# Zeros written by ScalarE, lambda powers placed by ScalarE copies, and one mask product for two heads

## The chip, the cores and the metric

The kernel runs on one core of a Trainium2 chip. Five engines work beside each other, each through its own queue in order: TensorE (PE, with its weight loads shown as PEld), VectorE (DVE), ScalarE (ACT), GpSimd (POOL) and SyncE (SP), which issues the DMAs. The metric is the device time of one execution in microseconds (us). The kernel before has a median of 950.24 us over three runs (948.44 to 950.54).

## The reference, cut to what matters

One decoder layer over 256 tokens of width 1024, in float32. The mixer makes one projection into S5 channels, q, k and v. Half of the channels go through a diagonal complex state space model, the other half through causal attention; their outputs meet in one output projection. Then follow a LayerNorm, a retrieval over 128 x 128 single-neuron experts (PEER), and a second LayerNorm.

```
proj = h @ w_in                                  # u | q | k | v
lam_bar = exp(lam * dt)                          # 32 groups x 64 complex states
bu = einsum('blgh,gph->blgp', u, b_bar)
states = scan(a1*a2, a2*b1 + b2)                 # over 256 tokens
y = real(einsum('blgp,ghp->blgh', states, c)) + d * u
y = gelu(y); y = y * sigmoid(y @ w_glu)
s = q @ k.T * scale;  s = where(k_pos <= q_pos, s, -1e30);  o = softmax(s) @ v
h = layernorm(alpha*h + concat(y, o) @ w_out)    # then PEER and a second layernorm
```

With 256 tokens and blocks of 256 there is only the own causal block, so the attention is plain causal attention over 8 heads of 64.

## The kernel before, in words

The tokens are permuted and stand in two blocks of 128 (b = 0 and 1). The S5 part works on chunks of 4 tokens: `Bbd` (128 x 2 x 16 x 4 x 32) holds the powers of lambda times B, and `Cbd` (128 x 2 x 16 x 5 x 32) those of lambda times C, both block diagonal over pairs of channel groups, so that zeros must stand off the diagonal. `Kin` (128 x 16 x 128) is the kernel within a chunk.

The mixer is a list of steps, `CFG["order"]` (line 46), emitted one after the other; a scheduler then sets the order on each engine. The steps that matter here are: `zero` (lines 666 to 671) fills `Bbd` on DVE, `Cbd` on POOL and `Kin` on ACT; `u` and `q` are projections whose products (lines 176 and 188) PE starts with; `par` makes the parameters on DVE, a long chain of operations on 128 x 16 tiles; `b` (from line 432) calls `powers` for `Bbd`; `min` (line 452) transposes `Bbd` on PE after the q projection; `c` calls `powers` for `Cbd`; `k` is the k projection as three products of split operands (`hi` and `lo`, lines 71 and 72); `e0`, `e1` (line 516) carry the inputs into chunk states; `v` (line 217) is the v projection in eight portions; `s0`, `s1` are the scans on DVE; `a0`, `a1` are `attend(0)` and `attend(1)`, four times each, with two heads a time; `kin` (line 498) makes `Kin`; `p0`, `p1` multiply with v; `o0`, `o1` read the states out; `glu` closes the S5 half.

`powers` forms, for the real and then the imaginary part, two products on DVE in full tiles (lines 421 and 422) and writes their difference or sum straight into the diagonal blocks, one instruction for each half of the partitions (line 426).

`attend` makes, for one of the two heads after the other, the score products (line 623: two recorded passes for each 128 x 128 block of keys) and adds the causal mask to the diagonal block by a product of an identity with the mask tile `mb` in bf16 (line 627). DVE takes the maximum (line 629), ACT the exponential (line 632), PE transposes the probabilities (line 637), ACT copies them out (line 639). The score banks (`pbank`) are four in number, the banks of the transposes (`abank`) two.

After the mixer come the output projection (line 768), the first LayerNorm, the retrieval's query products and the two long stages over the expert tables, in which PE works without a pause.

Of the kernel before, what the change touches and what calls it, by code (L numbers as in the profile page):

```python
# [14 lines left out]
AF = mybir.ActivationFunctionType  # L15
OP = mybir.AluOpType
# [6 lines left out]
NPAIR = 16  # L23
# [18 lines left out]
def f32(ap):  # L42
    return ap.bitcast(F32)


CFG = dict(order='mask zero u par b q min rt rot xs ks k c0 c vs e0 e1 s0 v v a0 v a0 v a0 a0 v s1 a1 v a1 v a1 a1 v kin p0 o0 p1 o1 glu',
           glu='VV',
           post='VV',
           yt='AAAAVVVVVVVPVVVV',
# [4 lines left out]
def layer(ctx, tc, I, out, tap=None, upto=None):  # L54
    nc = tc.nc
    V, S, P, PE = nc.vector, nc.scalar, nc.gpsimd, nc.tensor
# [24 lines left out]
    ident = const.tile([128, 128], F32, name="ident")  # L81
# [31 lines left out]
    with ExitStack() as px:  # L113
# [6 lines left out]
        with ExitStack() as mx:  # L120
# [14 lines left out]
            warm = se.tile([128, 512], F32, tag="yT", name="warm")  # L135
            V.memset(warm, 0.0)
            pt = pbank([128, 512])
# [30 lines left out]
            qk = sb.tile([128, 2, 4, T], F32, name="qk")  # L168
# [228 lines left out]
            Bbd = sb.tile([128, 2, NPAIR, 4, 32], F32, name="Bbd")  # L397
            Cbd = sb.tile([128, 2, NPAIR, 5, 32], F32, name="Cbd")
            MinT = sb.tile([128, 2, NPAIR, 128], F32, name="MinT")
            Kin = sb.tile([128, NPAIR, 128], F32, name="Kin")  # L400
            big = [se.tile([128, 1024], F32, name=f"big{n}") for n in range(4)]
            rot = sb.tile([128, 2, NPAIR, NCH], F32, name="rot")
# [5 lines left out]
            def powers(L, n, xr, xi, dst, k0, sg, EE, tmp):  # L408
                v = [b[:, :256 * n].rearrange("p (a k h) -> p a k h", k=n, h=16) for b in tmp]
                sh = [128, NPAIR, n, 16]  # L410
                lr, li = (L[:, i, :, :, None].to_broadcast(sh) for i in range(2))
                if sg < 0:
                    nl = sb.tile([128, NPAIR, n], F32, name="nl")
                    EE[1].tensor_scalar(nl, L[:, 0], -1.0, None, op0=OP.mult)
                    nlr = nl[:, :, :, None].to_broadcast(sh)
                xr, xi = (x[:, :, None, :].to_broadcast(sh) for x in (xr, xi))

                for i, (a, b) in enumerate(((xr, xi), (xi, xr))):
                    E = EE[i]
                    p, q = (v[(2 * i + k) % len(v)] for k in range(2))  # L420
                    E.tensor_tensor(p, a, nlr if i and sg < 0 else lr, op=OP.mult)
                    E.tensor_tensor(q, b, li, op=OP.mult)
                    for g in range(2):
                        sl = slice(64 * g, 64 * g + 64)
                        o = dst[sl, i, :, k0:k0 + n, 16 * g:16 * g + 16]
                        E.tensor_tensor(o, p[sl], q[sl],
                                        op=OP.add if i and sg > 0 else OP.subtract)

            bre, bim, cre, cim = (prm[:, 48 + 256 * n:304 + 256 * n].rearrange("p (a h) -> p a h", h=16)
                                  for n in range(4))  # L430
# [159 lines left out]
            mb = sb.tile([128, 128], BF, name="mb")  # L590
# [20 lines left out]
            def attend(b):  # L611

                nk = b + 1
                w = 128 * nk
                for n in range(4):

                    heads = [4 * (n // 2) + n % 2 + 2 * i for i in range(2)]
                    r = slice(64 * (n % 2), 64 * (n % 2) + 64)
                    pt = pbank([128, 2, T])
                    for i, h in enumerate(heads):  # L620
                        for kb in range(nk):
                            o = pt[:, i, 128 * kb:128 * kb + 128]
                            PE.matmul(o, qk[r, 0, h // 2, 128 * b:128 * b + 128],  # L623
                                      qk[r, 1, h // 2, 128 * kb:128 * kb + 128],
                                      start=True, stop=kb != b)
                            if kb == b:
                                PE.matmul(o, identb, mb, start=False, stop=True)
                    mx_ = sb.tile([128, 2], F32, tag="mx", bufs=2, name="mx_")
                    V.tensor_reduce(mx_, pt[:, :, :w], axis=AX.X, op=OP.max, negate=True)
                    p = sb.tile([128, 2, T], F32, tag="prob", bufs=2, name="p")  # L630
                    for i, h in enumerate(heads):
                        S.activation(p[:, i, :w], pt[:, i, :w], AF.Exp, bias=mx_[:, i:i + 1],
                                     accum_out=rs[:, b, h:h + 1])
                    pp = abank([128, 2, T])
                    for i in range(2):
                        for kb in range(nk):
                            PE.transpose(pp[:, i, 128 * kb:128 * kb + 128],
                                         p[:, i, 128 * kb:128 * kb + 128], ident)
                    S.copy(pTs[b][:, n], pp[:, :, :w])
                    yield  # L640
# [23 lines left out]

            def do(w):
                if w == "zero":
                    V.memset(Bbd, 0.0)
                    P.memset(Cbd, 0.0)
                    P.memset(Rt[:, :, 0:1], 0.0)
                    S.activation(Kin, ident[:, None, :].to_broadcast([128, NPAIR, 128]), AF.Copy,  # L670
                                 scale=0.0)
                elif w == "u":
                    pu = [abank([128, 512]) for _ in range(2)]
                    tokproj(0, pu)
                    for b in range(2):
                        V.transpose(U[:, :, b, :], pu[b].rearrange("p (a g) -> p a g", g=32))
                elif w == "q":
                    M["q"] = chproj(1, 0.125, lambda q: [(w_in(1, q), xT)])
                elif w == "k":
                    def parts(q):  # L680
                        hi, lo = M["wk", q]
                        return (hi, mixh), (hi, mixl), (lo, mixh)
                    chproj(2, 1.0, parts)
                elif w == "ks":
                    for q in range(4):
                        M["wk", q] = split(load(I["w_in"][2, :, 2 * q:2 * q + 2, :]), V)
                elif w == "vs":
                    vsplit()
                elif w == "xs":
                    xsplit()  # L690
                elif w == "v":

                    if "pv" not in M:
                        M["pv"] = [sbank([128, 512]) for _ in range(2)]
                        M["vproj"], M["left"] = vproj(M["pv"]), 8
                    next(M["vproj"])
                    M["left"] -= 1
                    if not M["left"]:
                        M["v"] = vn = sb.tile([128, 2, 512], F32, tag="vn", name="vn")
                        for b in range(2):  # L700
                            S.copy(vn[:, b], M["pv"][b])
                elif w == "par":
                    M["p"] = s5_params()
                elif w == "b":
                    s5_b(M["p"][0])
                elif w == "c0":
                    s5_c0()
                elif w == "c":
                    s5_c()
                elif w == "rt":  # L710
                    s5_rt(M["p"][1])
                elif w == "rot":
                    s5_rot()
                elif w == "min":
                    with tc.issue_after(M["q"].ins):
                        s5_min()
                elif w == "kin":
                    s5_kin()
                elif w in ("e0", "e1"):
                    M[w] = s5_e(int(w[1]))  # L720
                elif w in ("s0", "s1"):
                    if "S" not in M:
                        M["S"] = sb.tile([128, 2, NPAIR, NCH + 1], F32, tag="MinT", name="Sst")
                        P.memset(M["S"][:, :, :, 0:1], 0.0)
                    s5_scan(int(w[1]), M["e" + w[1]], M["S"])
                elif w in ("o0", "o1"):
                    if "y" not in M:
                        M["y"] = se.tile([128, 4, 2, 4, 32], F32, tag="yT", name="yT")
                    s5_out(int(w[1]), M["S"], M["y"])
                elif w == "mask":  # L730
                    masks()
                elif w in ("a0", "a1"):
                    if w not in M:
                        M[w] = attend(int(w[1]))
                    next(M[w])
                elif w in ("p0", "p1"):
                    values(int(w[1]), M["v"])
                elif w == "glu":
                    glu(M["y"])
                else:  # L740
                    raise ValueError(w)
# [101 lines left out]
            for q in range(4):  # L843
                raw = stream.tile([128, 1024], F32, tag="raw", bufs=RAWB, name="raw")
                for k in range(2):
                    c = 256 * q + 128 * k
# [518 lines left out]
```

## Time and profile before

| what | value |
|---|---|
| median of three runs | 950.24 us |
| the profiled execution's own time | 949.19 us |
| its span, from the first to the last instruction | 947.4 us |
| mean granted TensorE clock, as a share of full speed | 0.995 |
| PE busy | 935.1 us, 99% of the span |
| DVE, ACT and POOL busy | 722.2, 562.7 and 11.2 us |

Busy shares are means over stages with different limits. The first 125 us, to the end of the mixer, are the part that the change touches; DVE is nearly full there between 20 and 80 us. A TensorE matmul's end is modelled, so that rows of one engine overlap; the time from one row's start to the next one's start is what a step takes. A float32 product is recorded as two passes.

### The profile page before, as it was taken

What the parts mean: (1) busy time and instruction counts of PE and PEld (TensorE: products, weight loads), DVE (VectorE), ACT (ScalarE), POOL (GpSimd) and SP (SyncE); (2) the same over time, 40 slices, a digit from 0 to 9 for tenths busy, and PEclk for the clock granted to TensorE, in tenths of its full rate; (3) what the DMA queues carried; (4) which work ended last, traced back from release to release, by engine and by line L of the source; (5) the groups of instructions that cost most, each with busy time, mean ns of one, the idle gap of its engine ahead of it and who ended that gap; (6) DMA issues with size and microseconds to landing.
All of it is one profiled execution on the core that took longest, in us unless ns stands there. A gap on an engine that the chain in (4) does not pass through costs nothing.

```text
span 947.4 us, 15310 instructions
## 1 busy us (share of the span) xinstructions
PE 935.1 (99%) x5591; PEld 810.3 (86%) x5591; DVE 722.2 (76%) x1495; ACT 562.7 (59%) x1067; POOL 11.2 (1%) x19
## 2 busy tenths in 40 slices
PE   9999999999999999999999999999999999999996
PEld 4987889998888888999999999888888888888875
DVE  9998687998988967888898996655555555555566
ACT  4526544566575667998888776554455465445550
POOL 3000010000000000000000000000000000000000
PEclk9999999999999999999999999999999999999998
DMA  7331573455555555354444445555555575555561
GB/s 290 111 113 57 172 239 112 135 179 202 195 181 198 182 196 176 130 186 156 156 157 156 157 157 178 197 189 193 197 193 189 196 286 186 195 198 191 191 198 45
DMA packets 50075, 166.18 MB, mean 175 GB/s; under 512 B 5328, under 2 KB 9936, under 8 KB 49872
## 3 DMA queue, kind: packets, MB, share of 16 engines
q1 hardware_dynamic: 50000, 165.20, 51.7%
q8 instruction: 44, 0.72, 0.3%
q14 instruction: 31, 0.25, 0.1%
HBM read 163.09 MB, written 2.10 MB: 174 GB/s over the span
## 4 chain that ended last, share of the span: by engine, by line
PE 95%; DVE 4%; issue 0%; DMA 0%; ACT 0%; DVEq 0%; ACTq 0%
PE pg L1180 35%; PE pw L916 16%; PE pw L1268 10%; PE pw L918 10%; PE pg L1141 3%; PE pa L1268 3%; PE pw L919 2%; PE pw L768 2%; PE pw L188 2%; PE pa L176 2%; PE psb L217 1%; PE pa L871 1%; PE pw L623 1%; PE pw L498 1%; PE psb L552 1%; PE pw L648 1%
## 5 line engine op out<-in xcount | busy, mean ns | idle before, releaser
L72 DVE TENSOR_TENSOR lo<-raw,hi 128x1024 fp32r<-128x1024 f32 x167 | 204.4, 1224 | 150.7 <-ACT hi L71 150.4
L71 ACT CAST hi<-raw 128x1024 fp32r<-128x1024 f32 x167 | 175.9, 1054 | 169.6 <-PE pg L1180 153.9
L1180 PE MATMUL pg<-hi,wv 128*128 128x512 f32 x980 | 262.5, 389 | 0.5 <-ACT wv L1110 0.5
L1180 PEld LDWEIGHTS pg<-hi,wv 128*128 128x128 f32 x980 | 183.8, 188 | 39.0 <-ACT wv L1110 0.9
L916 PE MATMUL pw<-x,hi 128*128 128x512 f32 x672 | 171.2, 393 | 0.0
L1180 PE MATMUL pg<-lo,wv 128*128 128x512 f32 x490 | 151.1, 389 | 0.0
L916 PEld LDWEIGHTS pw<-x,hi 128*128 128x128 f32 x672 | 124.3, 189 | 23.2
L79 DVE TENSOR_TENSOR lo<-raw,hi 128x1024 fp32r<-128x1024 f32 x96 | 117.1, 1220 | 16.8 <-ACT hi L78 15.8
L918 PEld LDWEIGHTS pw<-x,lo 128*128 128x128 f32 x768 | 104.8, 190 | 7.4
L1180 PEld LDWEIGHTS pg<-lo,wv 128*128 128x128 f32 x490 | 92.0, 188 | 19.2
L918 PE MATMUL pw<-x,lo 128*128 128x256 f32 x768 | 107.3, 282 | 0.0
L78 ACT CAST hi<-raw 128x1024 fp32r<-128x1024 f32 x96 | 101.2, 1054 | 3.8 <-PE pa L1268 2.7
L921 ACT COPY ul<-pw 128x256 f32<-128x256 f32 x96 | 35.6, 371 | 90.0 <-PE pw L919 90.0
L1135 ACT ACTIVATE o<-eq,gL 128x128 f16<-128x128 f16 x256 | 84.3, 440 | 6.0 <-DVE eq L1131 5.6
L1268 PEld LDWEIGHTS pw<-x,hi 128*128 128x128 f32 x512 | 65.9, 189 | 1.3
L1268 PE MATMUL pw<-x,hi 128*128 128x256 f32 x512 | 66.6, 283 | 0.0
L1110 ACT CAST wv<-act 128x256 fp32r<-128x256 f32 x124 | 51.9, 419 | 0.8 <-DVE act L1147 0.8
L1111 DVE TENSOR_TENSOR wv<-act,wv 128x256 fp32r<-128x256 f32 x124 | 51.7, 418 | 0.0
L1268 PE MATMUL pw<-x,lo 128*128 128x256 f32 x256 | 38.8, 292 | 0.0
L919 PE MATMUL pw<-x,hi 128*128 128x512 f32 x96 | 38.0, 396 | 0.0
L1141 PE MATMUL pg<-o,o 128*128 128x128 f16 x512 | 36.5, 219 | 0.0
L922 DVE TENSOR_TENSOR us<-pw,ul 128x256 f32<-128x256 f32 x64 | 26.8, 418 | 11.6 <-ACT ul L921 10.9
(349 smaller groups left out, 1129.6 us busy)
## 6 DMA issues: line engine op xcount, KB each, us to landing
raw<-in_u SPq DMA_DIRECT2D x128, 512.0 KB, 3.5
raw<-in_v SPq DMA_DIRECT2D x128, 512.0 KB, 4.3
raw<-in_w_q SPq DMA_DIRECT2D x12, 512.0 KB, 4.3
raw<-in_w_in SPq DMA_DIRECT2D x8, 512.0 KB, 6.4
raw<-in_w_out SPq DMA_DIRECT2D x8, 512.0 KB, 4.2
w<-in_w_in SPq DMA_DIRECT2D x7, 512.0 KB, 9.4
raw<-in_w_q SPq DMA_DIRECT2D x8, 256.0 KB, 5.0
raw<-in_w_glu SPq DMA_DIRECT2D x2, 512.0 KB, 3.4
```

What stands on the lines that cost most here:

```text
L71: S.copy(hi, raw)
L72: eng.tensor_tensor(lo, raw, f32(hi), op=OP.subtract)
L78: S.copy(hi, raw)
L79: return hi, lo, V.tensor_tensor(lo, raw, f32(hi), op=OP.subtract)
L916: PE.matmul(pt, hi[:, 128 * d:128 * d + 128], x2[:, d], start=d == 0, stop=False)
L918: PE.matmul(pt[:, 0], lo[:, 128 * d:128 * d + 128], xh[:, d], start=False, stop=False)
L919: PE.matmul(pt, hi[:, D - 128:], x2[:, ND - 1], start=False, stop=True)
L1110: S.copy(wh, of_tile(half, i))
L1135: S.activation(o2[:, 1, i // 2, :, i % 2], eq[:, i // 2, :, i % 2], AF.Copy, scale=gL[:, t0 + i:t0 + i + 1])
L1141: PE.matmul(pt[:, i], o1[:, i // 2, :, i % 2], o2[:, k, i // 2, :, i % 2], start=k == 0, stop=k == 1)
L1180: PE.matmul(acc[b][:, c], x[:, tk], w[:, 512 * c:512 * c + 512], start=first and j == 0, stop=last and j == 2)
L1268: PE.matmul(pt, w[:, 128 * d:128 * d + 128], x[:, d], start=n == 0 and d == 0, stop=n == 2 and d == ND - 1)
```

## The change

`Bbd`, `Kin` and `Cbd` are filled by ACT copies from `warm`, a tile of zeros; the memset of `Bbd` leaves DVE and that of `Cbd` leaves POOL, and the fill of `Kin` no longer reads `ident`. The fill of `Cbd` is a step of its own (`zc`). In `powers` DVE makes one subtraction or addition over all partitions in place, and ACT copies the two halves into the diagonal blocks. In `attend` one mask product over both heads (128 x 2 x 128) comes first and opens the accumulation, and the score products of the diagonal block follow on top of it.

```diff
-CFG = dict(order='mask zero u par b q min rt rot xs ks k c0 c vs e0 ...
+CFG = dict(order='mask zero u par b q min rt rot xs zc ks k c0 c vs e0 ...
...
                     E.tensor_tensor(q, b, li, op=OP.mult)
+                    E.tensor_tensor(p, p, q, op=OP.add if i and sg > 0 else OP.subtract)
                     for g in range(2):
                         sl = slice(64 * g, 64 * g + 64)
-                        o = dst[sl, i, :, k0:k0 + n, 16 * g:16 * g + 16]
-                        E.tensor_tensor(o, p[sl], q[sl],
-                                        op=OP.add if i and sg > 0 else OP.subtract)
+                        S.copy(dst[sl, i, :, k0:k0 + n, 16 * g:16 * g + 16], p[sl])
...
-                    for i, h in enumerate(heads):
-                        for kb in range(nk):
-                            o = pt[:, i, 128 * kb:128 * kb + 128]
-                            PE.matmul(o, qk[r, 0, h // 2, 128 * b:128 * b + 128],
+                    for kb in range(nk):
+                        if kb == b:
+                            PE.matmul(pt[:, :, 128 * b:128 * b + 128], identb,
+                                      mb[:, None, :].to_broadcast([128, 2, 128]), start=True, stop=False)
+                        for i, h in enumerate(heads):
+                            PE.matmul(pt[:, i, 128 * kb:128 * kb + 128],
+                                      qk[r, 0, h // 2, 128 * b:128 * b + 128],
                                       qk[r, 1, h // 2, 128 * kb:128 * kb + 128],
-                                      start=True, stop=kb != b)
-                            if kb == b:
-                                PE.matmul(o, identb, mb, start=False, stop=True)
+                                      start=kb != b, stop=kb != b or i == 1)
...
                 if w == "zero":
-                    V.memset(Bbd, 0.0)
-                    P.memset(Cbd, 0.0)
+                    for z in (Bbd, Kin):
+                        o = z.rearrange("p a b c d -> p (a b c d)") if z is Bbd else z.rearrange("p a b -> p (a b)")
+                        S.copy(o.rearrange("p (n c) -> p n c", c=512),
+                               warm[:, None, :].to_broadcast([128, o.shape[1] // 512, 512]))
                     P.memset(Rt[:, :, 0:1], 0.0)
-                    S.activation(Kin, ident[:, None, :].to_broadcast([128, NPAIR, 128]), AF.Copy,
-                                 scale=0.0)
+                elif w == "zc":
+                    o = Cbd.rearrange("p a b c d -> p (a b c d)")
+                    S.copy(o.rearrange("p (n c) -> p n c", c=512),
+                           warm[:, None, :].to_broadcast([128, 10, 512]))
```

The scheduler moves instructions with it, up to the end of the mixer; behind that the order on every engine is the same. Three places follow.

On ACT at the start of the program, before:

```order
L670 ACT_TABLE_LOAD
L670 ACTIVATE Kin_127<-ident_61 128x2048
L199 CAST mixh_87<-x0_96 128x512
L485 COPY Rt_133<-pw_120 128x16x63
L199 CAST mixh_87<-x0_96 128x512
L378 COPY LamB_123<-Lam_122 128x32
L199 CAST mixh_87<-x0_96 128x512 x2
```

and in the changed kernel:

```order
L671 ACT_TABLE_LOAD
L671 COPY Bbd_124<-warm_98 128x4096
L671 COPY Kin_127<-warm_98 128x2048
L676 COPY Cbd_125<-warm_98 128x5120
L378 COPY LamB_123<-Lam_122 128x32 x2
L484 COPY Rt_133<-pw_120 128x16x63
L378 COPY LamB_123<-Lam_122 128x32
L199 CAST mixh_87<-x0_96 128x512 x4
```

Three fills of 4096, 2048 and 5120 columns stand in a row, and the copies of lambda and the casts of x come behind all three.

On PE behind the products of `e0` and `e1`, where before eight pairs of a score product and a mask product stood in a row (the last two and the first v products are shown; `psb` is the bank of the v projection):

```order
L627 LDWEIGHTS identb
L627 MATMUL pw<-mb,identb 128x128
L623 MATMUL pw<-qk 128x128
L627 LDWEIGHTS identb
L627 MATMUL pw<-mb,identb 128x128
L217 MATMUL psb<-hi,mixh 128x512
L217 MATMUL psb<-hi,mixl 128x512
L217 MATMUL psb<-lo,mixh 128x512
```

the changed kernel has:

```order
L515 MATMUL pa<-U,MinT 128x64 x16
L217 MATMUL psb<-hi,mixh 128x512
L217 MATMUL psb<-hi,mixl 128x512
L217 MATMUL psb<-lo,mixh 128x512
L217 MATMUL psb<-hi,mixh 128x512
L217 MATMUL psb<-hi,mixl 128x512
L217 MATMUL psb<-lo,mixh 128x512
L622 LDWEIGHTS identb
L622 MATMUL pw<-mb,identb 128x2x128
L625 MATMUL pw<-qk 128x128 x2
L217 MATMUL psb<-hi,mixh 128x512
L217 MATMUL psb<-hi,mixl 128x512
```

The v products now come first, and the four blocks of b = 0 (one mask, two scores) stand between them.

On ACT in the attention of b = 1 (`p` is a pair's probabilities, `vn` the copy of v, `x0` takes the transposed probabilities, `W5` is a tile of the output weights), before:

```order
L632 ACTIVATE p_769,rs_136<-pw_760,mx__767 128x256 x2
L701 COPY vn_850<-psb_658 128x512
L639 COPY x0_96<-pa_772 128x512
L632 ACTIVATE p_793,rs_136<-pw_784,mx__791 128x256 x2
L632 ACTIVATE p_817,rs_136<-pw_808,mx__815 128x256 x2
```

and in the changed kernel:

```order
L633 ACTIVATE p_768,rs_136<-pw_760,mx__766 128x256 x2
L71 CAST W5_1157<-raw_1158 128x1024
L640 COPY x0_96<-pa_771 128x512
L633 ACTIVATE p_791,rs_136<-pw_783,mx__789 128x256 x2
L633 ACTIVATE p_814,rs_136<-pw_806,mx__812 128x256 x2
```

The copy of v stood behind the first pair's exponentials; now the cast of `W5` stands there, which overwrites q and k and so waits for PE's last score product, and the copies of v come later.

## Rows read from the trace of the kernel before

**Rows 1.** The page: busy time of the engines, share of the span, instructions.

```profile
PE 935.1 (99%) x5591; PEld 810.3 (86%) x5591; DVE 722.2 (76%) x1495; ACT 562.7 (59%) x1067; POOL 11.2 (1%) x19
```

**Rows 2.** The waits of PE between 0 and 175 us: who waited for whom, us in total, times, the longest.

```profile
PE pa L1268 <- DVE lo L961: 0.6, 1, 0.6
PE psb L579 <- DVE yl L571: 0.4, 1, 0.4
PE psb L578 <- ACT yh L570: 0.3, 1, 0.3
```

**Rows 3.** The table of stretches: length, busy time of PE, PEld, DVE, ACT and POOL with instructions in brackets, granted clock, DMA share, GB/s.

```profile
55.00:60.00 5.00, 5.00 (x34) 3.90 (x32) 4.96 (x6) 1.05 (x1) 0.15 (x1) 1.00 0.49 143
60.00:65.00 5.00, 5.00 (x18) 3.82 (x18) 5.00 (x8) 0.00 (x0) 0.00 (x0) 0.66 0.50 172
75.00:80.00 5.00, 5.00 (x31) 3.51 (x29) 4.61 (x8) 3.49 (x16) 0.00 (x0) 1.00 0.00 0
```

**Rows 4.** PE in order of time in the k projection: start us, modelled duration us, what.

```profile
46.44 0.28 PE L188 MATMUL pw<-mixl,hi 128*128 128x256 f32 x1
46.80 0.39 PE L188 MATMUL pw<-mixh,lo 128*128 128x256 f32 x1
47.03 0.28 PE L188 MATMUL pw<-mixh,hi 128*128 128x256 f32 x1
```

**Rows 5.** PE in order of time, scores and masks of b = 0, then the first v products.

```profile
57.15 0.23 PE L627 MATMUL pw<-mb,identb 128*128 128x128 bf16 x1
57.30 0.48 PE L623 MATMUL pw<-qk 64*128 64x128 f32 x2
57.72 0.23 PE L627 MATMUL pw<-mb,identb 128*128 128x128 bf16 x1
...
61.22 0.56 PE L217 MATMUL psb<-hi,mixh 128*128 128x512 f32 x1
...
62.43 0.63 PE L217 MATMUL psb<-hi,mixh 128*128 128x512 f32 x1
62.86 0.63 PE L217 MATMUL psb<-hi,mixl 128*128 128x512 f32 x1
...
64.95 0.39 PE L217 MATMUL psb<-hi,mixh 128*128 128x512 f32 x1
65.18 0.40 PE L217 MATMUL psb<-hi,mixl 128*128 128x512 f32 x1
```

**Rows 6.** PE in order of time, one pair of heads of b = 1 and the v products behind it.

```profile
69.88 0.71 PE L623 MATMUL pw<-qk 64*128 64x128 f32 x4
70.52 0.23 PE L627 MATMUL pw<-mb,identb 128*128 128x128 bf16 x1
70.68 0.71 PE L623 MATMUL pw<-qk 64*128 64x128 f32 x4
...
71.36 0.48 PE L217 MATMUL psb<-wv,mixh 128*128 128x512 f32 x1
71.67 0.41 PE L217 MATMUL psb<-wv,mixl 128*128 128x512 f32 x1
```

**Rows 7.** DVE in order of time: the fill of `Bbd`, two of the first parameter operations, and the first operation of step `b`.

```profile
2.20 3.47 DVE L667 MEMSET Bbd<- 128x4096 f32 x1 [0.80 <-issue]
...
6.36 1.49 DVE L245 TENSOR_SCALAR pw<-pw 128x16 f32<-128x16 f32 x1
...
8.70 0.17 DVE L245 TENSOR_SCALAR pw<-pw 128x16 f32<-128x16 f32 x1
...
19.12 0.41 DVE L436 TENSOR_TENSOR big<-prm,pw 128x256 f32<-128x256 f32 x1
```

**Rows 8.** POOL in order of time.

```profile
1.93 4.36 POOL L668 MEMSET Cbd<- 128x5120 f32 x1
...
6.29 1.53 POOL L748 IOTA iotaq<- 128x256 f16 x1
7.76 0.46 POOL L750 IOTA iotal<- 128x256 bf16 x1
```

**Rows 9.** The parameters' first DMA on SP (start us, us) and, from the list of DMA issues up to 60 us, size and us from issue to landing.

```profile
1.65 0.42 SPq L146 DMA_DIRECT2D prm<-in_prm  x1
prm<-in_prm SPq DMA_DIRECT2D x1, 24.0 KB, 2.5
```

**Rows 10.** ACT's table load, its fill of `Kin` and two placing copies of half the partitions, and DVE's placing of powers in `Bbd`, in order of time.

```profile
0.74 1.28 ACT L670 ACT_TABLE_LOAD   x1 [0.74 <-PEq L1354]
10.38 1.91 ACT L670 ACTIVATE Kin<-ident 128x2048 f32<-128x2048 f32 x1 [8.36 <-DVE ident L96]
23.31 0.82 ACT L444 COPY Bbd<-Bc 64x256 f32<-64x256 f32 x2 [1.92 <-DVE Bc L441]
28.55 1.91 DVE L426 TENSOR_TENSOR Bbd<-big,big 64x768 f32<-64x768 f32 x2
```

**Rows 11.** PE's first transposes of `Bbd`; ACT in the attention of b = 1, a copy of transposed probabilities and the second pair's first exponential; PE's transposes of one pair's probabilities.

```profile
33.49 1.04 PE L452 MATMUL psb<-ident,Bbd 128*128 128x128 f32 x8
81.58 0.59 ACT L639 COPY x<-pa 128x512 f32<-128x512 f32 x1
82.06 0.49 ACT L632 ACTIVATE p<-pw,mx__791 128x256 f32<-128x256 f32 x1
80.90 0.60 PE L637 MATMUL pa<-ident,p 128*128 128x128 f32 x4
```

More of the change, by code (lines that the diff above doesn't have):

```diff
@@ L43, in f32 @@
     return ap.bitcast(F32)
-CFG = dict(order='mask zero u par b q min rt rot xs ks k c0 c vs e0 e1 s0 v v a0 v a0 v a0 a0 v s1 a1 v a1 v a1 a1 v kin p0 o0 p1 o1 glu',
+CFG = dict(order='mask zero u par b q min rt rot xs zc ks k c0 c vs e0 e1 s0 v v a0 v a0 v a0 a0 v s1 a1 v a1 v a1 a1 v kin p0 o0 p1 o1 glu',
            glu='VV',
```

## The prediction

> **What bounds the kernel now.** I read the page first: PE is busy 99% of the span, every other engine less [rows 1]. The list of PE's waits comes second. Up to 175 us, past its start, it holds only three short ones, 0.6, 0.4 and 0.3 us [rows 2]. So PE is the bound nearly everywhere, and DVE and ACT count only where they make PE wait. Busy time does not show steps that are longer than they need be; for that I read, third, the table of stretches, where the granted clock is 0.66 between 60 and 65 us, while PE is busy all the time [rows 3]; and fourth, PE in order of time, measuring from one start to the next. The reader is to see three things there.
>
> First, in the k projection one step takes 46.80 - 46.44 = 0.36 us and the next 0.23, where its neighbours take 0.12 (47.03 to the next row and the rows ahead show it as an even beat): 0.24 + 0.10 = 0.34 us are a short wait for `lo`, which DVE makes late [rows 4]. Second, the v products step by 62.86 - 62.43 = 0.43 us at first and by 65.18 - 64.95 = 0.23 later; that is the lower of the clock's two levels (1.2 GHz) against the upper (2.4 GHz) [rows 5]. Third, a score product behind a mask takes 57.72 - 57.30 = 0.42 us for its two passes, a mask 57.30 - 57.15 = 0.15, together 0.57 for a head of b = 0 [rows 5]; with four passes (b = 1) the scores take 0.64 and the head 70.68 - 69.88 = 0.80 [rows 6]. Two more passes thus cost only 0.22: half of the 0.42 is the change between score and mask.
>
> **The change part by part.** The sum is made against the profiled execution, 949.19 us (span 947.4), which is 1.05 us under the median of 950.24.
>
> *One mask for two heads.* Eight of 16 masks go. A pair of b = 0 costs 2 x 0.57 = 1.14 now. Then it is a mask, a score behind a mask (0.42) and one behind a score (0.22). A mask of 256 columns is not in the trace; it is at least the 0.15 of 128 columns, and at most 0.21 if 128 more columns cost a quarter of the 0.23 us that 512 take. That is 0.79 to 0.85, a gain of about 0.3 each. A pair of b = 1 costs 71.36 - 69.88 = 1.48 now; then 0.64 for the two heads' first block of keys, and 0.79 to 0.85 less the 0.1 that is saved where no mask follows the last score: 1.33 to 1.39, a gain of about 0.1. Four of each: 4 x 0.3 + 4 x 0.1 = 1.6. Against that stand the changes between v products and scores: the four b = 0 blocks now stand at three places instead of one (the order shows it), and the first v step behind scores is 71.67 - 71.36 = 0.31 rather than 0.23 [rows 6]; with the way in I take 0.05 to 0.15 for each of two more. I take 1.5 in all; bounds -0.3 (nothing gained in the pairs, the switches paid) and 2.9 (0.36 for each of eight).
>
> *The clock.* The v products from 61.22 to 65.18 are ten steps in 3.96 us; at 0.23 they would be 2.3, so 1.7 us are lost [rows 5]. What PE did before the clock fell was eight pairs of score and mask in a row, half of the rows of the array in use (64*128). The stretch ahead, 55 to 60 us, has 1.00, and so has the one with b = 1 scores, from 75 to 80 [rows 3]. In the changed order v products at 512 columns stand ahead of and between the b = 0 blocks, and the blocks are denser. I take the fall as gone: 1.7; bounds 0 (it stays) and 1.7. The Trainium skill ("TensorE: Matmul & The Clock Gate", HAM oscillation — how this bites in real kernels) has gaps in which PE idles bring the clock down. By that rule the fall has no cause here, since PE is busy throughout, and the edit could not remove it: the sum would be 1.8 instead of 3.5. The trace differs from it, with 5.00 of 5.00 us busy at a clock of 0.66, so I go by the order of the work.
>
> *Zeros.* DVE's memset of 3.47 us goes, POOL's of 4.36 too [rows 7, 8]. DVE's parameter chain now starts at 2.20 + 3.47 = 5.7 us, behind the memset, and its first operations are stretched: one of 16 columns takes 1.49 us where a like one takes 0.17, and ends at 7.85, just as POOL's iota does (6.29 + 1.53 = 7.82) [rows 7, 8]. In the changed kernel POOL is through with its iotas at about 4 us (1.93, where the memset started, + 1.53 + 0.46), and the parameters land at 1.65 + 2.5 = 4.15 [rows 9]. So the chain runs from 4.15 without a stretch, and step `b` starts at about 15 instead of 19.12 us: DVE is 4 us ahead. On ACT the fills cost 1.91 / 2048 us a column [rows 10]: 3.8 + 1.9 + 4.8 = 10.5 us from the end of the table load at 2.02, so to 12.5 us; now the fill of `Kin` ends at 12.3, because it waits for `ident`. Nothing is late by it. Cost nothing; without that cover the copies of lambda would take from DVE's 4 us, not from PE.
>
> *Powers.* DVE saves half of its placing, 1.91 / 2 for each of two parts of `Bbd` [rows 10], and for `Cbd` 4/3 of that, having 1024 columns for 768: 1.9 + 2.5 = 4.4 us. ACT gets eight copies of 64 partitions; a placing of 256 columns takes 0.82 / 2 = 0.41 [rows 10], and with 512 and 768 more columns at the fill's rate they take 0.9 and 1.1, together 8 us. ACT has room: 1.05 us busy of 5 from 55 to 60, 0 from 60 to 65 [rows 3]. For PE `Bbd` must be whole at 33.49 [rows 11]; today DVE ends it at 30.46, then, 4 us earlier with a copy of 1.8 behind, at about 28. Cost nothing; if the cover of 5 us went, each further microsecond would be PE's. DVE then reaches `lo` in the k projection some 4 us earlier, and the wait of 0.34 goes. What is late next is PE itself.
>
> *ACT's queue in the attention.* The cast of `W5` (1.05) now waits for PE's last score product, and behind it stand a copy of 0.48 (82.06 - 81.58 [rows 11]) and the second pair's exponentials of 0.45. They reach PE 2.0 us after the last score. PE has four transposes (0.60 with a modelled end [rows 11], so 0.4 to 0.6), six v products (6 x 0.23) and two of `kin` (as the two passes of a score, 0.22 each, an estimate) until it needs them: 2.2 to 2.4. It fits by 0.2 to 0.4 us. Cost nothing; if it slips, up to 1.
>
> *Downstream.* The order behind the mixer is the same. The two waits of 0.4 and 0.3 in `glu` [rows 2] hang on the end of the S5 output, which moves with PE; they stay.
>
> Sum: 1.5 + 1.7 + 0.34 = 3.5. 949.19 - 3.5 = 945.7 for an execution like the profiled one; with the 1.05 to the median, 946.7.
>
> **The rivals.**
>
> *The clock still falls*, at the same place or at another one. For it: PE was never idle before, so I know only one instance of the cause; the b = 0 blocks still end with two in a row. Against it: the v products between. 950.24 - 1.8 = 948.4.
>
> *The gain is given back at the end of the mixer.* PE comes 3.5 us earlier to `glu` and the output projection, and finds weights or the chain from S5 output to `yl` not ready. For it: PE already waits there, on DVE and ACT [rows 2]. Against it: those loads are issued when DVE has finished with a buffer, and DVE is ahead. 950.2, no change.
>
> *ACT becomes the bound at the end of the attention.* The cast stands at the head of the queue and three pairs wait behind it. If PE had to wait for each pair's copy and exponentials in full (0.48 + 0.9), that is 3 x 1.4 + 1.05 = 5.2 us, and in such a lull the clock could fall, 1.7 more: 950.24 - 3.5 + 6.9 = 953.6. It decides from 3.5 us of such waiting on; against it stand the 0.2 to 0.4 us of room, and that all four pairs' score banks are filled by then.
>
> **How the numbers follow.** Forecast 0.62, clock falls 0.17, given back 0.12, ACT bound 0.09. A measurement of this kernel tells 0.2% from no change, 1.9 us: faster is under 948.34, slower over 952.14. The forecast is faster in nine of ten of its cases (its own spread is that of the mask, about 1 us, and of the runs, about 1), the clock case lies on the bound and is faster in half. Faster: 0.56 + 0.085 = 0.65; slower 0.09; the same 0.26. The range: best case 2.9 + 1.7 + 0.34 = 4.9 and the lowest run 1.8 below the median give no more than 943.5; above it reaches past the given-back case, 950.6, and leaves out the slower one.
>
> **What would show it.** Right: eight mask rows of 128x256 with steps near 0.8 us for a block of b = 0; a clock of 1.00 in all stretches from 55 to 70 us; step `b` on DVE at about 15 us; an even beat of 0.12 in the k projection; the last score product some 3.5 us earlier, and the output projection as well. Wrong: PE waits on the exponentials or on `Bbd`, a lower clock anywhere in the mixer, or an output projection that starts where it did.

## The result and the profile after

The changed kernel takes 945.33 us (median of five runs, 945.16 to 945.89) where the kernel before, run beside it, takes 950.44 (948.44 to 950.67). The ratio is 0.9949, with a 95% interval of 0.9938 to 0.9961: 5.1 us, or 0.5%, faster. The prediction was 946.7 us, so the direction and the range held and the time came out 1.4 us lower. The two profiled executions stand closer: 949.19 against 945.52, a gain of 3.67 where 3.5 was forecast. Why the medians are further apart than the profiles is the question of one of the experiments; in a later comparison the medians were 949.24 (15 runs) and 945.50, 3.7 us apart.

The page of the changed kernel: the span, and busy time, share and instructions of each engine, which answer to [rows 1].

```profile
span 943.7 us, 15299 instructions
PE 931.6 (99%) x5583; PEld 807.3 (86%) x5583; DVE 712.9 (76%) x1490; ACT 578.1 (61%) x1077; POOL 6.9 (1%) x18
```

PE has eight products fewer, the eight masks. DVE lost 9.3 us and ACT gained 15.4, and neither difference is in the time as such.

The waits of PE between 0 and 175 us in the changed kernel, which answer to [rows 2]:

```profile
PE pa L1274 <- DVE lo L967: 0.6, 1, 0.6
PE psb L578 <- DVE yl L570: 0.4, 1, 0.4
PE psb L577 <- ACT yh L569: 0.3, 1, 0.3
```

They are the same three with the same sizes; no new wait has come. The table of stretches of the changed kernel (busy PE, PEld, DVE, ACT, POOL, granted clock, DMA share, GB/s), beside [rows 3]:

```profile
55.00:60.00 5.00, 5.00 (x29) 4.07 (x29) 5.00 (x8) 0.00 (x0) 0.16 (x1) 1.00 0.50 190
60.00:65.00 5.00, 5.00 (x26) 3.53 (x25) 3.46 (x8) 3.27 (x9) 0.00 (x0) 1.00 0.01 3
```

The 0.66 between 60 and 65 us has become 1.00. PE in order of time in the changed kernel (start, modelled duration): its first product at line 188, the k projection, the first v product, the first block of b = 0, the last two, a pair of b = 1 followed by v products, two pairs of b = 1 one behind the other, and the first product of the output projection.

```profile
19.41 1.67 PE L188 MATMUL pw<-x,w 128*128 128x256 f32 x7
...
46.78 0.28 PE L188 MATMUL pw<-mixh,hi 128*128 128x256 f32 x1
46.90 0.28 PE L188 MATMUL pw<-mixl,hi 128*128 128x256 f32 x1
...
56.00 0.48 PE L217 MATMUL psb<-hi,mixh 128*128 128x512 f32 x1
...
57.46 0.28 PE L622 MATMUL pw<-mb,identb 128*128 128x256 bf16 x1
57.67 0.71 PE L625 MATMUL pw<-qk 64*128 64x128 f32 x4
58.31 0.50 PE L217 MATMUL psb<-hi,mixh 128*128 128x512 f32 x1
58.65 0.39 PE L217 MATMUL psb<-hi,mixl 128*128 128x512 f32 x1
...
63.53 0.28 PE L622 MATMUL pw<-mb,identb 128*128 128x256 bf16 x1
...
64.38 0.28 PE L622 MATMUL pw<-mb,identb 128*128 128x256 bf16 x1
...
66.83 0.71 PE L625 MATMUL pw<-qk 64*128 64x128 f32 x4
...
68.32 0.50 PE L217 MATMUL psb<-wv,mixh 128*128 128x512 f32 x1
...
73.88 0.71 PE L625 MATMUL pw<-qk 64*128 64x128 f32 x4
74.52 0.28 PE L622 MATMUL pw<-mb,identb 128*128 128x256 bf16 x1
74.73 0.72 PE L625 MATMUL pw<-qk 64*128 64x128 f32 x8
75.39 0.28 PE L622 MATMUL pw<-mb,identb 128*128 128x256 bf16 x1
...
76.24 0.44 PE L638 MATMUL pa<-ident,p 128*128 128x128 f32 x2
...
105.32 0.39 PE L774 MATMUL pw<-hi,mixh 128*128 128x512 f32 x1
```

The reader is to see five things. The k projection keeps its beat of 0.12. A mask for two heads takes 57.67 - 57.46 = 0.21, a block of b = 0 64.38 - 63.53 = 0.85. The first v step behind scores takes 58.65 - 58.31 = 0.34. A pair of b = 1 followed by v takes 68.32 - 66.83 = 1.49, no less than the 1.48 of [rows 6]; two pairs one behind the other take 76.24 - 73.88 = 2.36, and the eight score passes that stand between their masks take 75.39 - 74.73 = 0.66, where four take 74.52 - 73.88 = 0.64. And the output projection starts at 105.32.

The kernel before, PE in order of time, at the same two ends and at three marks between them (the first score of b = 0, a mask of b = 1 ahead of v, the first v product behind the last score):

```profile
19.67 1.24 PE L188 MATMUL pw<-x,w 128*128 128x256 f32 x5
...
56.73 0.49 PE L623 MATMUL pw<-qk 64*128 64x128 f32 x2
...
71.32 0.23 PE L627 MATMUL pw<-mb,identb 128*128 128x128 bf16 x1
...
80.12 0.48 PE L217 MATMUL psb<-hi,mixh 128*128 128x512 f32 x1
...
108.96 0.42 PE L768 MATMUL pw<-hi,mixh 128*128 128x512 f32 x1
```

From the first product at line 188 to the output projection both kernels do the same work but for the eight masks. That length, called the stretch from here on, leaves out the start, where PE waits for the first weights by a different amount in each execution. It was 108.96 - 19.67 = 89.29 us and is 105.32 - 19.41 = 85.91: 3.38 of the 3.67 us. Behind it nothing changed.

DVE, POOL and ACT in order of time in the changed kernel: DVE's first parameter operation and the first product of step `b` (at line 435), POOL's two operations that stood behind its memset, ACT's fills, the last placing in `Bbd`, and the cast of `W5` (recorded as `W`) with what follows it.

```profile
4.17 0.17 DVE L245 TENSOR_SCALAR pw<-prm 128x16 f32<-128x16 f32 x1 [2.77 <-DMA prm<-in_prm]
...
15.41 0.43 DVE L435 TENSOR_TENSOR big<-prm,pw 128x256 f32<-128x256 f32 x1
```

```profile
1.99 1.53 POOL L754 IOTA iotaq<- 128x256 f16 x1
3.46 0.46 POOL L756 IOTA iotal<- 128x256 bf16 x1
```

```profile
2.03 3.60 ACT L671 COPY Bbd<-warm 128x4096 f32<-128x4096 f32 x1
5.54 1.89 ACT L671 COPY Kin<-warm 128x2048 f32<-128x2048 f32 x1
7.34 4.45 ACT L676 COPY Cbd<-warm 128x5120 f32<-128x5120 f32 x1
...
24.86 1.68 ACT L426 COPY Bbd<-big 64x768 f32<-64x768 f32 x2 [0.16 <-DVE big L423]
...
76.35 1.05 ACT L71 CAST W<-raw 128x1024 fp32r<-128x1024 f32 x1 [1.06 <-PE pw L625]
77.30 0.58 ACT L640 COPY x<-pa 128x512 f32<-128x512 f32 x1
77.78 0.48 ACT L633 ACTIVATE p<-pw,mx__789 128x256 f32<-128x256 f32 x1
```

The parameter chain starts at 4.17 without a stretched operation, step `b` at 15.41 instead of 19.12 [rows 7], and `Bbd` is whole at 24.86 + 1.68 = 26.5 us.

### The profile page after: what moved, and what is told of

It is laid out like the page before. It is cut to its first block, busy times and chain, and to the rows that moved or that the text cites. A ratio compares the mean times of both kernels' runs of the same rounds, so it can differ in the third digit from the quotient of the medians.

```text
span 943.7 us, 15299 instructions
## 1 busy us (share of the span) xinstructions
PE 931.6 (99%) x5583; PEld 807.3 (86%) x5583; DVE 712.9 (76%) x1490; ACT 578.1 (61%) x1077; POOL 6.9 (1%) x18
## 4 chain that ended last, share of the span: by engine, by line
PE 96%; DVE 3%; DMA 0%; issue 0%; ACT 0%; DVEq 0%; ACTq 0%
PE pg L1186 35%; PE pw L922 16%; PE pw L1274 10%; PE pw L924 10%; PE pg L1147 3%; PE pw L188 3%; PE pa L1274 3%; PE pw L925 2%; PE pw L774 2%; PE pa L176 2%; PE psb L217 1%; PE pa L877 1%; PE pw L497 1%; PE pw L625 1%; PE psb L551 1%; PE pw L649 1%
```

## The experiments

Eight more kernels ran, and four runs repeated a kernel. The theory to test was the prediction's own: masks and clock make the gain, zeros and powers only move DVE. The rivals: the relief of DVE is the gain; or the order of the products is, whatever the masks. The table gives the stretch of each profiled execution, the granted clock between 60 and 65 us in it, and the median of all runs; the texts below take the rows one by one. A ratio is taken against runs of the kernel before beside it, whose medians were 950.42 us (masks alone, zeros and powers, and both kernels with the blocks put in a row), 949.78 (the other four) and 949.24 (the repeats).

| kernel | b = 0 blocks stand | stretch, us | granted clock, 60 to 65 us | median (runs), us | ratio to before, 95% |
|---|---|---|---|---|---|
| before | in a row | 89.29 | 0.66 | 950.44 (5) | |
| changed | between v products | 85.91 | 1.00 | 945.33 (5) | 0.9938 to 0.9961 |
| masks alone | in a row | 87.71 | 1.00 | 947.89 (11) | 0.9973 to 0.9991 |
| masks, zeros | in a row | 86.66 | 1.00 | 947.05 (9) | 0.9963 to 0.9983 |
| masks, powers | between | 85.91 | 1.00 | 946.34 (5) | 0.9949 to 0.9976 |
| zeros alone | in a row | 90.39 | 0.50 | 949.20 (11) | 0.9987 to 1.0005 |
| zeros, powers | between | 88.10 | 1.00 | 948.21 (11) | 0.9978 to 0.9996 |
| zeros, powers, blocks put in a row | in a row | 89.50 | 0.66 | 949.97 (11) | 0.9993 to 1.0011 |
| changed, blocks put in a row | in a row | 87.17 | 0.67 | 944.59 (5) | 0.9930 to 0.9957 |
| changed, blocks two and two | two places | 86.01 | 1.00 | 946.22 (5) | 0.9949 to 0.9976 |

**The masks alone**, on the kernel before:

```diff
-                    for i, h in enumerate(heads):
-                        for kb in range(nk):
...
+                    for kb in range(nk):
+                        if kb == b:
+                            PE.matmul(pt[:, :, 128 * b:128 * b + 128], identb,
+                                      mb[:, None, :].to_broadcast([128, 2, 128]), start=True, stop=False)
...
```

> The kernel before with the one mask product for two heads alone; zeros and powers as before, so DVE stays late and the four b = 0 blocks stand in a row behind e0 and e1. All theories: the masks save about 1.6 us in the pairs. If the clock falls because scores and masks stand in a row (order), it falls here too and the time is 950.4 - 1.6 = 948.8 us. If it fell because single mask products leave the array too thin (density), the denser blocks keep the clock up and the time is 950.4 - 1.6 - 1.7 = 947.1 us.

It took 947.89 us, ratio 0.9982, between the two values expected. In its profile the clock is at 1.00, although the blocks stand in a row, but PE is idle. The stretch between 60 and 65 us, PE, and DVE in order of time:

```profile
60.00:65.00 5.00, 4.02 (x18) 3.30 (x18) 5.00 (x8) 1.06 (x1) 0.00 (x0) 1.00 0.48 167
```

```profile
59.38 0.71 PE L626 MATMUL pw<-qk 64*128 64x128 f32 x4
61.08 0.47 PE L217 MATMUL psb<-hi,mixh 128*128 128x512 f32 x1 [0.98 <-DVE big L527]
```

```profile
54.30 2.45 DVE L426 TENSOR_TENSOR Cbd<-cp 64x1024 f32<-64x1024 f32 x2
...
60.25 0.68 DVE L527 TENSOR_TENSOR big<-psb,rot 128x512 f32<-128x512 f32 x1
```

The first v product needs a bank that DVE empties at line 527, and DVE came late to it, among other things because it was still placing the powers of `Cbd` (2.45 us at line 426). The step from 59.38 to 61.08 takes 1.70 us, where four passes take 0.64; without these 1.06 us the stretch would be 86.65.

**Masks and zeros, masks and powers, zeros alone.** Each is a part of the change undone or done: the memsets put back (masks and powers), the difference written straight into the blocks again (masks and zeros), and the zeros put alone on the kernel before.

```diff
-                elif w == "zc":
-                    o = Cbd.rearrange("p a b c d -> p (a b c d)")
...
+                    V.memset(Bbd, 0.0)
+                    P.memset(Cbd, 0.0)
...
```

```diff
-                    E.tensor_tensor(p, p, q, op=OP.add if i and sg > 0 else OP.subtract)
...
-                        S.copy(dst[sl, i, :, k0:k0 + n, 16 * g:16 * g + 16], p[sl])
+                        o = dst[sl, i, :, k0:k0 + n, 16 * g:16 * g + 16]
+                        E.tensor_tensor(o, p[sl], q[sl],
+                                        op=OP.add if i and sg > 0 else OP.subtract)
```

> The kernel before with one mask for two heads and with the zeros by ScalarE, but the powers still placed by DVE. The masks alone left PE waiting 1.05 us for the bank of the first v product, which DVE's scan frees late. If the zeros' 4 us of DVE are what removes that wait, no PE wait is left between 55 and 65 us and the time is 944.6 us (the blocks stand in a row, as in rowpair) or 947 where the clock falls. If the powers' 4.4 us on DVE are needed for it, a wait of 0.5 us or more stays and the time is 946 us or more.

> One mask for two heads and the powers placed by ScalarE, zeros as before, so DVE starts its parameters at 5.7 us and under GpSimd's memset. If any 4 us of DVE ahead of the scan remove the wait, there is none here either and the time is that of the changed kernel, 945.3 us. If the late start matters, Bbd comes 4 us later than in the changed kernel (about 30 us, still ahead of 33.5) and lo in the k projection late again: 945.3 + 0.3 = 945.6 us.

> The zeros by ScalarE alone. PE-bound theory: PE saves only the 0.34 us wait in the k projection, the single scores and masks stand in a row and the clock falls: 950.4 - 0.3 = 950.1 us, no change that can be told. Rival, DVE is the bound up to the scan: 4 us of DVE come out as 2 us or more, 948.4 us or less.

Masks and zeros took 947.05 us with a stretch of 86.66, that of the masks alone less PE's wait to 0.01: DVE, ahead by the zeros, no longer keeps PE waiting. Yet 944.6 us had been expected without a wait and a fall; what is missing lies in the order, below. Masks and powers took 946.34, with a stretch of 85.91, the changed kernel's to the hundredth. (The median is 1.0 us above the changed kernel's; but on the same chip the order two and two, with the zeros by ScalarE, took 946.22.) So beside the powers the zeros are worth nothing in the stretch, and either of the two is enough to cover what the masks uncover. The powers do one thing more. In the kernels without them the scheduler puts the four blocks in a row behind `e1`; in the kernels with them, masks or not, it puts v products first and between. (The powers alone were not run.) They also order the attention of b = 1 otherwise: with masks and zeros, transposes stand between the score passes of a pair; with masks and powers, as in the changed kernel, eight passes of two pairs stand in one run. From the first score of b = 1 to the first product of `kin` the one takes 12.47 us and the other 11.38; the interleaved blocks ahead of it give back 10.82 - 10.46 = 0.36. The kernel before, without its fall (1.7) and its wait for `lo` (0.34), has a stretch of 87.25. So in the order without the powers the masks are worth only 87.25 - 86.66 = 0.6 us.

Zeros alone took 949.20 us, no difference. Its profile has a longer fall of the clock than the kernel before, in the stretches from 55, 60 and 65 us:

```profile
55.00:60.00 5.00, 5.00 (x29) 3.64 (x28) 5.00 (x8) 0.00 (x0) 0.15 (x1) 0.93 0.66 200
60.00:65.00 5.00, 5.00 (x14) 3.78 (x14) 4.19 (x8) 0.00 (x0) 0.00 (x0) 0.50 0.02 10
65.00:70.00 5.00, 5.00 (x21) 4.05 (x20) 2.02 (x5) 3.49 (x10) 0.00 (x0) 0.89 0.02 5
```

**Zeros and powers; the same with the blocks in a row; the changed kernel with the blocks in a row, and two and two.** The first puts the masks for one head back, and the others change the list of steps, the first list for the blocks in a row and the second for two and two:

```diff
-CFG = dict(order='mask zero ... vs e0 e1 s0 v v a0 v a0 v a0 a0 v s1 ...
+CFG = dict(order='mask zero ... vs e0 e1 a0 a0 a0 a0 s0 v v v v v s1 ...
```

```diff
-CFG = dict(order='mask zero ... vs e0 e1 s0 v v a0 v a0 v a0 a0 v s1 ...
+CFG = dict(order='mask zero ... vs e0 e1 a0 a0 s0 v v v a0 a0 v v s1 ...
```

> The changed kernel with the two single masks put back; zeros and powers stay with ScalarE, so the v products come first and the single scores and masks stand between them. If the order makes the clock fall, it stays at 1.00 here, the k projection has no wait (0.34 us), and the time is 950.4 - 2.0 + 0.2 for two more switches = 948.6 us. If density makes it fall, it still falls somewhere between 57 and 65 us and the time is 950.1 us. If all of the gain came from the masks, 950.4 us.

> As zeropow (zeros and powers by ScalarE, single masks), but the steps a0 are emitted in a row ahead of the first v step, so that the eight pairs of score and mask stand in a row again while DVE is early. If the stretch of scores and masks makes the clock fall, it falls here with DVE 4 us ahead: about 1.7 us over zeropow, 950.1 us. If DVE's lateness or chance made it fall, no stretch shows under 1.00 and the time equals zeropow's, 948.6 us or less.

> The changed kernel with the four b = 0 blocks in a row ahead of the first v step, and nothing else moved. Order theory: the clock falls as before, 945.3 + 1.7 - 0.2 for fewer switches = 946.8 us. Density theory: the blocks with one mask for two heads keep the clock at 1.00, and the time is 945.3 us or 0.2 less.

> The changed kernel with two of the four b = 0 blocks ahead of the first v step and the other two one by one between the v steps. If only the switches count, there is one way in from v less than in the changed kernel: 945.2 us. If two blocks behind e0 and e1 are enough to let the clock fall, 1.7 more: 946.9 us, and a stretch with 0.66 in the profile.

Zeros and powers took 948.21 us, and with the blocks put in a row 949.97. Their stretches between 60 and 65 us, the interleaved one first:

```profile
60.00:65.00 5.00, 5.00 (x24) 3.29 (x23) 2.92 (x6) 3.02 (x8) 0.00 (x0) 1.00 0.00 0
```

```profile
60.00:65.00 5.00, 5.00 (x17) 3.93 (x17) 4.87 (x7) 0.00 (x0) 0.00 (x0) 0.66 0.01 3
```

DVE is early in both, PE is busy in both, and only the place of the eight blocks differs: the row of scores and single masks goes with the fall, not DVE's lateness. From the interleaved one to the changed kernel only the masks differ: 88.10 - 85.91 = 2.19 us. With the blocks in a row, both with one fall of the same length, it is 89.50 - 87.17 = 2.33.

The changed kernel with its blocks in a row was not clear. Its profiled execution, at 946.93 us, had the fall (the first of the two rows below); the other four lay between 944.40 and 945.14. It ran again:

> The changed kernel with its four b = 0 blocks in a row, profiled once more. Theory A (the row of thin products brings the fall on, but not in every execution; without a fall the row is 0.5 us cheaper than the products between): most executions 944.4 to 945.2, some near 947, and a profile without a fall shows 1.00 from 55 to 80 us, the four blocks in 3.4 us, and the first step of the output projection some 85.4 us after the first of the input projection at line 188, where the changed kernel has 85.9. Theory B (the one profile with a fall was no more than a chance event that any of these kernels can have): no execution near 947, or as many of the changed kernel.

> The changed kernel, unchanged, on the chip of the next kernel. Both theories: median 945.0 to 945.9, clock 1.00 from 55 to 80 us. If the fall only became rarer, and did not go, some executions lie near 947 with a mean clock of 0.995 or 0.996 and a longer time; if the interleaved products keep it up, all of them lie within 0.8 us.

The second time, none of five executions stood out (945.11 to 945.76, median 945.33), and the profile has no fall (the second row):

```profile
60.00:65.00 5.00, 5.00 (x16) 3.96 (x16) 5.00 (x9) 0.00 (x0) 0.00 (x0) 0.67 0.01 3
```

```profile
60.00:65.00 5.00, 5.00 (x23) 4.14 (x23) 5.00 (x8) 1.05 (x1) 0.00 (x0) 1.00 0.02 3
```

No execution near 947 is what theory B had named as its sign, and one fall in ten executions is too little to tell the theories apart; but the same program can fall or not. On the same chip the changed kernel took 945.50 us (945.17 to 945.90), all five without a fall in their times. The stretch of the row without a fall is 85.58, 0.33 less than 85.91, where 0.5 was expected, and the medians are no different: there is no version here that beats the change. The order two and two has 86.01 and 946.22 us, between the values expected, with no fall in its profile, and gains nothing either.

**The kernel before, twice more**, for the difference between the profile of 949.19 us and the median:

> The kernel before, unchanged, profiled once more. Its executions so far lie near 949.1 us (mean granted clock 0.995, as in the profile shown: one stretch at half speed, 61.5 to 64.9 us) and near 950.5 (mean 0.994). Theory A: the upper ones are executions in which the half-speed stretch is twice as long, about 6.8 us as in the profile of the kernel with the zeros alone; a profile of 950.5 shows a clock near 0.5 for the whole of 60 to 65 us and some of 65 to 70, and v products at 0.43 us throughout. Theory B: the 1.3 us lie elsewhere (the first weights' DMA, PE's first step at 20 us); a profile of 950.5 then shows 0.66 in 60 to 65 us, as before, and a later first projection step. A profile of 949 decides nothing by itself.

> The kernel before, a third profile, for the same question as the second: near 949.1 one half-speed stretch of 3.4 us, near 950.5 one of 6.8 us (theory A), or the same 3.4 us and the difference elsewhere (theory B).

The first came at 950.41 us, with this table of stretches and PE in the k projection:

```profile
55.00:60.00 5.00, 5.00 (x32) 3.83 (x31) 4.96 (x6) 1.04 (x1) 0.16 (x1) 0.89 0.48 143
60.00:65.00 5.00, 5.00 (x16) 3.61 (x16) 5.00 (x8) 0.00 (x0) 0.00 (x0) 0.50 0.50 171
65.00:70.00 5.00, 5.00 (x22) 4.06 (x21) 3.68 (x8) 2.77 (x10) 0.00 (x0) 0.92 0.02 5
```

```profile
45.95 0.28 PE L188 MATMUL pw<-mixl,hi 128*128 128x256 f32 x1
46.80 0.39 PE L188 MATMUL pw<-mixh,lo 128*128 128x256 f32 x1 [0.57 <-DVE lo L72]
```

The second came at 948.46, with 0.66 between 60 and 65 us. Theory A holds: an execution near 950.5 spends about twice as long at half speed, (1 - 0.89) x 10 + 5 + (1 - 0.92) x 10 = 6.9 us against (1 - 0.66) x 10 = 3.4. The profile at 950.41 and the one at 949.19 both leave the wait for `lo` at 46.80 us, and from there to the output projection they take 110.26 - 46.80 = 63.46 and 108.96 - 46.80 = 62.16: the longer fall costs 1.3 us more. Of the kernel before, 72 executions of these experiments fall into two groups by their mean clock, and the groups do not overlap in time: 34 with 0.995 or 0.996, from 948.42 to 949.31 us, and 38 with 0.993 or 0.994, from 949.74 to 950.96.

## Why the prediction was right, and where its sizes were off

**One mask for two heads** was put at 1.5 us, and the sum came out close. By profiles it was 37.06 - 36.59 - 0.34 (the wait for `lo`) = 0.13 from the first product at line 188 to the first one behind `e1`, 13.15 - 1.7 (the fall) - 10.83 = 0.62 from there to the first score of b = 1 (56.73 to 69.88 before, 56.00 to 66.83 after), 10.24 - 9.41 = 0.83 to the end of the scores (80.12 before, 76.24 after), less 29.08 - 28.84 = 0.24 behind it: 1.3 us. That this is close is luck, for two errors cancel: the masks are worth more than 1.6, and the new order costs more than the 0.1 to 0.3 of the switches.

The order first. The kernel before, without fall and wait, has 87.25; the zeros and powers, with single masks in the new order, 88.10: 0.85 us. The place of the b = 0 blocks is 0.3 of it, as the switches were put (88.10 - (89.50 - 1.7) = 0.30 with single masks, 85.91 - 85.58 = 0.33 with masks for two heads). The rest lies behind them, in the attention of b = 1 and `kin`, and the prediction put nothing there.

Then the masks, 2.19 in that order (88.10 - 85.91). Between the first product behind `e1` and the first score of b = 1 the zeros and powers take 11.86 us and the changed kernel 10.83: 1.03 for b = 0, where 4 x 0.3 was put, with a block at 0.85, the upper of the two values given. From that score to `kin` they take 12.54 and 11.39: 1.15 for b = 1, where 4 x 0.1 was put. The term that was mis-sized is the pair of b = 1 at 1.33 to 1.39. Ahead of v products it gained nothing, because the 0.1 that was to be saved behind the last score does not exist: a mask ended in a v product within 71.36 - 71.32 = 0.04 before, while v behind scores now needs 0.34 for its first step. The gain of b = 1 comes where pairs follow each other, at 1.18 a pair. The kernel puts them on different halves of the array's rows in turn (`r = slice(64 * (n % 2), ...)`), and with no mask between them the passes of the two pairs start in twos, 0.01 us apart, so that eight take 0.66 us.

**The clock.** The fall of 1.7 us is gone, as forecast, and in none of ten executions of the changed kernel does the time show one. What it hangs on is partly settled. The row of eight scores with a mask each brought the fall in every profile (kernel before three times, zeros alone, and zeros and powers in a row). The denser row with masks for two heads brought it in one of the two profiles of the changed kernel with its blocks in a row, and in neither of two others (masks alone; masks and zeros); five of those two kernels' 20 executions lie 1.2 to 1.7 us above their medians, as a fall would put them. Single masks between v products did not fall in the profile, though two of eleven executions lie 1.3 and 1.9 us above the median. With both, none of 20 executions of the three kernels (changed, masks and powers, two and two) stands out. So, judged by times where no profile was taken, each of the two parts makes the fall rarer; that both together do more than either rests on these few executions. The prediction, which named both, did not say that one of them alone might not do. Why one execution of a program falls and the next does not stays open.

The Trainium skill ("TensorE: Matmul & The Clock Gate", HAM oscillation — how this bites in real kernels) lets gaps in which PE idles bring the clock down. The traces show a fall without such a gap: the clock fell with PE busy 5.00 of 5.00 us. With the masks alone PE was idle for 1.06 us and the clock stayed at 1.00; no run here has a longer gap in this part, so what longer ones do is not tested.

**The median** is where the time was missed by 1.4 us. The step that failed is the last one, "with the 1.05 to the median, 946.7". It carried the distance between the profile and the median over as something that the change leaves alone. It was the second half of the fall, 1.3 us, and went with the first. The gain by medians, 5.1 us, is large for a further reason: by their times four of the five runs of the kernel before had the longer fall, against 38 of 72 later.

**Zeros and powers** cost nothing, as forecast, and the covers held: `Bbd` is whole at 26.5 us, before PE needs it. The wait of 0.34 for `lo` is gone. It ends at 46.80, 46.80 and 46.83 us in the three profiles of the kernel before, whose first products at line 188 differ by 0.5 us (19.67, 19.17 and 19.59): there DVE set the time, and an earlier start was lost again. "What is late next is PE itself" holds for the change as a whole and not for its parts: with the masks alone DVE was next, for 1.06 us. The zeros are thus no gain by themselves (0.9996) but a cover of the masks' gain. The powers cover it too, and brought about the order: with single masks that order costs 0.85 us but makes the fall rarer (0.9987 for zeros and powers), and with masks for two heads it raises what the masks are worth from 0.6 to 2.2.

**ACT's queue** fitted. The cast starts at 76.35, right behind the last score product, and the second pair's exponentials at 77.78; no wait of PE is in the list. The rival of ACT as the bound falls, and so does the one of the gain given back: the two waits in `glu` are where they were, and the output projection starts 3.6 us earlier, 3.4 counted from line 188.

## What to carry to other kernels

Measure a stage between two products of the bound engine that stand on either side of it, rather than by the whole time alone: a start that varies by 1 us hides what a change of 1 us does. When a profile and the median of the same kernel differ, look for the reason before carrying the difference over; here it was part of the loss that the change removes. And when PE gets shorter, ask for each part of the change which engine was just in time before: relief that is worth nothing alone can be what keeps another part's gain. Compare the order on the bound engine as well: here the same edit was worth 0.6 us in one order and 2.2 in another.

## What was not expected of the hardware

The granted clock fell to half speed, 0.50, while PE was busy without a gap, behind a row of eight scores, with 64 of 128 rows of the array in use, and eight bf16 masks: the lower of its two levels, 1.2 GHz for 2.4. It stayed there for about 3.4 us in some executions of the same program and about 6.9 in others, and in one program it fell in one execution of ten. Between products of different kinds PE loses time that no wait shows: a v product's first step behind scores takes 0.34 us instead of 0.23, the two passes of a score behind a mask of 128 columns 0.42 instead of 0.22. And score passes on different halves of the rows, next to each other in the queue, overlap: eight take 0.66 us, where four on one half take 0.64.
